# Retention's result turned by VectorE in 32x32 blocks that change places through HBM, with the second attention's branch behind the third gate

## The chip, the cores and the metric

The kernel runs on one core of a Trainium2 chip. The metric is device time in microseconds (us) of one execution; lower is better. Three timed executions of the kernel before gave 818.8, 818.8 and 819.42 us, median 818.8.

## What is computed

A decoder trunk of two layers over 256 tokens of width 1024. In each layer three token mixers run side by side on the normed input: MLA attention, MoBA attention (here one block, so plain causal attention) and retention. Each mixer's result goes through a matrix of its own (its branch), is scaled by a gate of its own, and the three are summed and sent through `w_out`:

```python
merged = (jax.nn.sigmoid(g_mla) * (o_mla @ w_branch_mla)
          + jax.nn.sigmoid(g_moba) * (o_moba @ w_branch_moba)
          + jax.nn.sigmoid(g_ret) * (o_ret @ w_branch_ret))
return merged @ w_out
```

Retention ends in a group norm over each head's 128 columns, a gain and bias, and a silu gate. Then follow a residual, a norm, a squared-ReLU MLP of width 4096 and another residual; after both layers a final norm.

## The kernel before

**Tiles.** The 256 tokens are two row tiles (`t` = 0, 1) of 128 partitions. A matmul contracts over partitions, so whatever is multiplied by a weight must stand turned: features on partitions, tokens along the free axis. Products are of fp32 accuracy: every operand is split into a rounded high part and the rest (`hi`, `lo`), and `three` (L239 to L242) issues three matmuls of 128x512 for each pair.

**Weights.** A weight block (512 KB for most) is loaded by SP into one of seven `raw` buffers (`fetch`, L204), copied by ScalarE into `whi` (L219) and subtracted by VectorE into `wlo` (L221), six buffers each. Every weight block costs each of these two engines one instruction of about a microsecond.

**Order of the work.** `prog` is a list of units that TensorE runs in turn: the three `project` calls of retention (`rqk`, `rv`, `rg`), the branch of MoBA (`bmoba`, two halves of 512 output columns in two units each), the third gate (`gret`, two halves in four units), the branch of retention (`bret`), then `w_out`. Steps hung on a unit with `at(slot(...))` are called behind it in program order. Within that a scheduler with a timeline model sets each engine's order, and each engine then runs its own queue strictly in that order.

**Retention's end.** `ret_values` (L1021 to L1023) leaves the result in two PSUM tiles `por`. `group_norm` takes statistics (L1033, L1034), a power -0.5 on GpSimd (L1036), normalises row tile 0 on VectorE (L1047) and row tile 1 on ScalarE (L1045), and applies gain, bias and gate in two VectorE instructions per row tile (L1051, L1052). The result `oret` stands in rows. `oret_turn` turns it: eight TensorE transposes of 128x128 per layer into PSUM tiles `pot` (L1061), and two splits into `oreth` (ScalarE) and `oretl` (VectorE), L261.

**The branches' sum.** `branch` (L630) multiplies by the branch's weights and then, on VectorE, gates each of four tiles (half, t) with a SCALAR_TENSOR_TENSOR (L650, which also frees the PSUM tile `acc`) and adds it to `merged` (L651). `merged_turn` (L1091, called between the matmuls of `bret1`, whose TensorE order is written out by hand) transposes `merged` on TensorE, four transposes `pmt` (L1097) per tile, for `w_out`.

**The MLP's own turn.** `squared_relu` (L1185) turns its hidden tile in another way: VectorE turns 32x32 blocks (STREAM_TRANSPOSE, L1192), one DMA stores them to a `bounce` buffer in HBM (L1194), four DMAs read them back with the blocks in their new places (L1198), and ScalarE and VectorE split the result (L261). There are eight such trips per layer.

Of the kernel before, what the change touches and what calls it, by code (L numbers as in the profile page):

```python
# [7 lines left out]
F32 = mybir.dt.float32  # L8
# [6 lines left out]
P = 128  # L15
D = 1024
S = 256
NT = S // P
L = 2
KD = D // P  # L20
DFF = 4096
NF = DFF // P

ENDS = [2] * (L - 1) + [4]
LEAD = 10
# [35 lines left out]
def weight_plan():  # L61

    plan = []

    def block(key, name, kt, cols, per):
        for j in range(0, kt, per):
            plan.append(((*key, j // per), name, (j, per), cols))

    def turned(key, cols):
        for n in range(4):  # L70
            block((*key, n), "w_in", KD, cols[P * n : P * n + P], KD)

    def span(c, n):
        return range(c, c + n)

    for l in range(L):
        if l == 0:

            for i in range(2):
                plan.append(((l, "mq", i), "w_in", (0, 1), C_MQ[256 * i : 256 * i + 256]))  # L80
            plan.append(((l, "b0", 0), "w_in", (0, 1), C_MLA))
            for k in range(1, KD):
                plan.append(((l, "b0mq", k), "w_in", (k, 1), [*C_MLA, *C_MQ]))
        else:
            block((l, "b0"), "w_in", KD, C_MLA, 2)
            turned((l, "mq"), C_MQ)
        turned((l, "mk"), C_MK)
        block((l, "mv"), "w_in", KD, C_MV, 2)
        mv, plan = plan[-4:], plan[:-4]
        for i, (key, name, kt, cols) in enumerate(  # L90
            (("qrope", "mla_w_q_up", 2, C_QROPE), ("qnope", "mla_w_q_up", 2, C_QNOPE), ("kvup", "mla_w_kv_up", 1, C_KV))
        ):
            block((l, key), name, kt, cols, kt)
            plan.append(mv[i])
        plan.append(mv[3])
        for i in range(2):
            block((l, "gmla%d" % i), "w_in", KD, span(C_GMLA + 512 * i, 512), 2)
        for i in range(2):
            block((l, "gmoba%d" % i), "w_in", KD, span(C_GMOBA + 512 * i, 512), 2)
        for i in range(2):  # L100
            block((l, "bmla%d" % i), "w_branch_mla", 4, span(512 * i, 512), 2)
        turned((l, "rqk"), C_RQK)
        block((l, "rv"), "w_in", KD, C_RV, 2)
        block((l, "rg"), "w_in", KD, span(C_RG, 512), 2)
        for i in range(2):
            block((l, "bmoba%d" % i), "w_branch_moba", 4, span(512 * i, 512), 2)
        for i in range(2):
            block((l, "gret%d" % i), "w_in", KD, span(C_GRET + 512 * i, 512), 2)
        for i in range(2):
            block((l, "bret%d" % i), "w_branch_ret", 4, span(512 * i, 512), 2)  # L110
        for n in range(KD):
            block((l, "wout", n), "w_out", KD, span(P * n, P), KD)
        for kind, i in mlp_order():
            if kind == "up":
                g, j = divmod(i, 4)
                plan.append(((l, "up", g, j), "w_mlp_up", (2 * j, 2), span(512 * g, 512)))
            else:
                plan.append(((l, "down", i, 0), "w_mlp_down", (i, 1), range(D)))
    at, offset = {}, 0
    for key, name, (j, n), cols in plan:  # L120
        at[key] = (offset, n, len(cols))
        offset += P * n * len(cols)
    return plan, at, offset
# [22 lines left out]
def trunk(ctx: ExitStack, tc: tile.TileContext, gx, wts, consts, gfin, gn, xtok, out):  # L146
# [83 lines left out]
    def misc_tile(name="misc"):  # L230
        return ps.tile([P, 512], F32, name=name, tag="misc", bufs=4)
# [4 lines left out]
    def t4(name):  # L236
        return sb.tile([P, 4, S], F32R, name=name, tag="t4", bufs=T4)
# [24 lines left out]

    def chunk(n):
        return X[n // 4][:, n % 4, :]

    class Normed:

# [359 lines left out]
            project(l, f"{key}{half}", xn, 512, lambda accs, half=half: done(half, accs))  # L627
        return th

    def branch(l, key, oT, th, merged, between=None):  # L630


        def unit(half, j, accs):
# [19 lines left out]
                    merged[half, t] = z  # L653
                    nc.vector.scalar_tensor_tensor(z, z, 1.0, accs[t], op0=ALU.add, op1=ALU.mult)

        for half in range(2):
            accs = []
            for j in range(2):
                prog.append(((f"{key}{half}", j), lambda half=half, j=j, accs=accs: unit(half, j, accs)))
# [46 lines left out]
    def at(slot, step):  # L706
        steps.setdefault(slot, []).append(step)
# [12 lines left out]
    def layer(l, xn, before):  # L720
# [241 lines left out]

        at(slot("gmoba1", 3), load_dec)
        merged, mT = {}, []
        branch(l, "bmla", omlaT, th_mla, merged)
        if l == 0:

            for i, (key, j) in enumerate((("gmoba0", 0), ("gmoba0", 1), ("gmoba1", 0), ("gmoba1", 1))):
# [29 lines left out]
                rqkv["tab"] = tables(xn, rqkv["dec"][:, RT_H * 3 * P :], nc.gpsimd)  # L998
            rT.append(rope_turned(raw, rqkv["tab"], nc.vector))

        rT, or_ps, aT, rg, oret = [], [], {}, {}, []

        def ret_scores():
            banks = [misc_tile("ps_r") for _ in range(RT_H)][::-1]
# [46 lines left out]
                nc.vector.scalar_tensor_tensor(o, o, xn.halfcol[t], gw, op0=ALU.mult, op1=ALU.mult)  # L1051
                nc.vector.scalar_tensor_tensor(o, gb, xn.halfcol[t], o, op0=ALU.mult, op1=ALU.add)  # L1052

        def oret_turn(i):
            if i == 0:
                oretT.extend((t4("oreth"), t4("oretl")))
            pt = misc_tile("pot")
            for kk in range(2):
                k = 2 * i + kk
                for t in range(NT):  # L1060
                    nc.tensor.transpose(  # L1061
                        pt[:, (2 * kk + t) * P : (2 * kk + t + 1) * P], oret[t][:, P * k : P * k + P], ident
                    )
            split_plain(pt, *(o[:, 2 * i : 2 * i + 2, :].rearrange("p k s -> p (k s)") for o in oretT))

        project_turned(l, "rqk", xn, ret_pair)
        project(l, "rv", xn, 512, ret_done("rv"))
# [16 lines left out]

        project(l, "rg", xn, 512, rg_done)
        at(slot("rg", 0), load_gn)
        branch(l, "bmoba", omobaT, th_moba, merged)
        th_ret = gates(l, "gret", xn)
        order_out = ExitStack()

# [15 lines left out]
            else:  # L1106
                merged_turn(0, i - 1)

        branch(l, "bret", oretT, th_ret, merged, between)
        at(slot("rg", 1), lambda: in_a_row(*moba_last, ret_scores))  # L1110
        for h in range(RT_H):
            at(slot("rg", 3), lambda h=h: ret_values(h))
        at(slot("rg", 3), group_norm)
        for i in range(2):
            at(slot("gret0", 3), lambda i=i: oret_turn(i))


        xm = []
# [65 lines left out]

        def squared_relu(g):  # L1185

            blocks = sb.tile([P, 4 * S], F32, name="hblocks", tag="probT", bufs=2)
            for t in range(NT):
                s = w2k("relu")
                nc.scalar.activation(s, us[g][t], AF.Relu, scale=xm.col[t])  # L1190
                nc.scalar.activation(s, s, AF.Square)
                nc.vector.transpose(blocks.rearrange("p (b j t e) -> p t j b e", b=4, j=4, t=2)[:, t], s)  # L1192
            bounce = dr.tile([P, 4 * S], F32, name="hbounce", bufs=2)
            nc.sync.dma_start(bounce, blocks)  # L1194
            turned = sb.tile([P, 4 * S], F32, name="hturned", tag="t4", bufs=T4)
            for b in range(4):
                src = bounce.rearrange("(a p) (b r) -> b p a r", a=4, b=4)[b]
                nc.sync.dma_start(turned[32 * b : 32 * b + 32, :].rearrange("p (a r) -> p a r", a=4), src)  # L1198
            sq = sb.tile([P, 2, 4, S], F32R, name="sq", tag=("Q", "KK")[g % 2], bufs=1)
            src = turned.rearrange("p (a m e) -> p m a e", a=4, e=32)  # L1200
            dst = (sq[:, i].rearrange("p j (t a e) -> p (j t) a e", a=4, e=32) for i in range(2))
            latest[:] = split_plain(src, *dst)
            for j in range(4):
                h2[4 * g + j] = sq[:, 0, j, :], sq[:, 1, j, :]

# [227 lines left out]
```

## Time and profile before

| | before |
|---|---|
| median of three timed runs | 818.8 us |
| the profiled execution, its own time | 819.33 us |
| its span, first to last instruction | 817.2 us |
| TensorE (PE) busy | 810.5 us, 99% |
| VectorE (DVE) busy | 573.4 us, 70% |
| ScalarE (ACT) busy | 459.8 us, 56% |
| GpSimd (POOL) busy | 97.1 us, 12% |
| mean granted TensorE clock | 0.998 |

The profile is of one execution. Busy shares are means over all stages; what limits a stage is read from the stretch itself, and for TensorE from how far apart its matmuls start, since they overlap. Times inside a layer are from the span's start. The two layers repeat the stage that the change touches; the second stands 403.19 us behind the first (its first `bmoba` matmul starts at 563.46, the first layer's at 160.27).

### The profile page before, as it was taken

The page shows a single profiled execution, that of the slowest core. Times are in us where ns is not written, and L with a number is a line of the kernel's source. Part 1 is how long each engine was busy: PE and PEld are TensorE (multiplying, and loading weights), DVE is VectorE, ACT ScalarE, POOL GpSimd, SP SyncE. Part 2 cuts the span into 40 slices and gives each one's busy share as a digit, 9 for nine tenths or more (in the row PEclk, how much of TensorE's full clock was granted, in tenths as well). Part 3 has the DMA queues.
Part 4 walks back from the last instruction along what each step waited for, and adds up shares of the span by engine and source line. Part 5 has one row for each costly group of instructions (what it writes and reads, how often), then busy time and mean ns, then how long its engine had stood idle before and what let it go on. Part 6 is the DMA issues. An engine that isn't in the chain of part 4 may idle for free.

```text
span 817.2 us, 11451 instructions
## 1 busy us (share of the span) xinstructions
PE 810.5 (99%) x4023; PEld 679.8 (83%) x4023; DVE 573.4 (70%) x940; ACT 459.8 (56%) x724; POOL 97.1 (12%) x75
## 2 busy tenths in 40 slices
PE   9999999999999999999999999999999999999997
PEld 7888888888888888888898888888888888888885
DVE  6879699796786455555597976787978744565562
ACT  7676655445555455555586565554555544565552
POOL 0100540330030000000035210013201200000000
PEclk9999999999999999999999999999999999999999
DMA  9964665757476777777656548548575776777731
GB/s 335 346 238 131 243 205 182 265 202 222 143 224 213 241 254 271 249 249 235 205 185 206 190 132 332 165 120 288 163 232 164 242 233 223 257 258 257 243 118 51
DMA packets 62648, 177.94 MB, mean 218 GB/s; under 512 B 8704, under 2 KB 21376, under 8 KB 62336
## 3 DMA queue, kind: packets, MB, share of 16 engines
q1 hardware_dynamic: 61248, 175.77, 64.4%
q10 hardware_dynamic: 1344, 1.46, 0.6%
q8 instruction: 31, 0.51, 0.2%
q14 instruction: 25, 0.20, 0.1%
HBM read 159.37 MB, written 9.44 MB: 207 GB/s over the span
## 4 chain that ended last, share of the span: by engine, by line
PE 99%; DVE 0%; ACT 0%; issue 0%; DVEq 0%
PE acc L242 18%; PE acc L240 18%; PE acc L241 18%; PE pup L241 7%; PE pup L242 7%; PE pup L240 7%; PE acc L1131 5%; PE acc L421 5%; PE acc L423 2%; PE ps_s L947 1%; PE acc L789 1%; PE po L588 1%; PE ps_s L490 1%; PE warm L700 0%; PE acc L791 0%; PE po L590 0%
## 5 line engine op out<-in xcount | busy, mean ns | idle before, releaser
L221 DVE TENSOR_TENSOR wlo<-raw,whi 128x1024 fp32r<-128x1024 f32 (+4 forms) x287 | 342.4, 1212 | 113.1 <-ACT whi L219 110.2
L219 ACT ACTIVATE whi<-raw 128x1024 fp32r<-128x1024 f32 (+4 forms) x287 | 287.6, 1022 | 168.3 <-PE acc L242 92.5
L240 PE MATMUL acc<-whi,xs 128*128 128x512 f32 (+1 forms) x304 | 118.7, 392 | 0.0
L242 PE MATMUL acc<-whi,xs 128*128 128x512 f32 (+1 forms) x304 | 118.4, 390 | 0.0
L241 PE MATMUL acc<-wlo,xs 128*128 128x512 f32 (+1 forms) x304 | 117.8, 387 | 0.0
L240 PE MATMUL acc<-whi,sq 128*128 128x512 f32 x256 | 99.9, 390 | 0.0
L241 PE MATMUL pup<-wlo,xs 128*128 128x512 f32 x256 | 99.8, 390 | 0.0
L242 PE MATMUL pup<-whi,xs 128*128 128x512 f32 x256 | 99.6, 389 | 0.0
L242 PE MATMUL acc<-whi,sq 128*128 128x512 f32 x256 | 99.6, 389 | 0.0
L241 PE MATMUL acc<-wlo,sq 128*128 128x512 f32 x256 | 99.6, 389 | 0.0
L240 PE MATMUL pup<-whi,xs 128*128 128x512 f32 x256 | 99.3, 389 | 0.0
L261 DVE TENSOR_TENSOR sq<-hturned,sq 128x1024 fp32r<-128x1024 f32 x16 | 19.6, 1225 | 77.6 <-ACT sq L261 77.6
L242 PEld LDWEIGHTS acc<-whi,xs 128*128 128x128 f32 x304 | 57.1, 188 | 11.5
L240 PEld LDWEIGHTS acc<-whi,xs 128*128 128x128 f32 x304 | 57.0, 188 | 11.5 <-issue 0.7
L241 PEld LDWEIGHTS acc<-wlo,xs 128*128 128x128 f32 x304 | 57.1, 188 | 10.9
L261 ACT ACTIVATE sq<-hturned 128x1024 fp32r<-128x1024 f32 x16 | 17.0, 1061 | 80.9 <-DMA hturned<-hbounce 80.9
L240 PEld LDWEIGHTS acc<-whi,sq 128*128 128x128 f32 x256 | 48.1, 188 | 10.0
L242 PEld LDWEIGHTS acc<-whi,sq 128*128 128x128 f32 x256 | 48.0, 188 | 10.0
L242 PEld LDWEIGHTS pup<-whi,xs 128*128 128x128 f32 x256 | 48.1, 188 | 9.8
L241 PEld LDWEIGHTS acc<-wlo,sq 128*128 128x128 f32 x256 | 48.1, 188 | 9.8
L241 PEld LDWEIGHTS pup<-wlo,xs 128*128 128x128 f32 x256 | 48.1, 188 | 9.8
L240 PEld LDWEIGHTS pup<-whi,xs 128*128 128x128 f32 x256 | 47.9, 188 | 9.8
(218 smaller groups left out, 1136.7 us busy)
## 6 DMA issues: line engine op xcount, KB each, us to landing
raw<-wts SPq DMA_DIRECT2D x264, 512.0 KB, 4.6
hbounce<-hblocks SPq DMA_DIRECT2D x16, 512.0 KB, 4.5
hturned<-hbounce SPq DMA_DIRECT2D x64, 128.0 KB, 2.9
probT<-blocks SPq DMA_DIRECT2D x80, 48.0 KB, 1.9
qkoth<-qkraw SPq DMA_DIRECT2D x48, 64.0 KB, 2.3
raw<-wts SPq DMA_DIRECT2D x5, 464.0 KB, 6.0
dec<-consts SPq DMA_DIRECT2D x2, 1024.0 KB, 6.3
raw<-wts SPq DMA_DIRECT2D x4, 416.0 KB, 4.1
```

Source lines behind the costliest of these rows:

```text
L219: nc.scalar.activation(hi[:, cs], raw[:, cs], AF.Copy)
L221: nc.vector.tensor_sub(lo[:, cs], raw[:, cs], hi[:, cs].bitcast(F32))
L240: nc.tensor.matmul(o, ah, bh, start=start, stop=False)
L241: nc.tensor.matmul(o, ah, bl, start=False, stop=False)
L242: nc.tensor.matmul(o, al, bh, start=False, stop=stop)
L261: return nc.scalar.activation(hi, src, AF.Copy), nc.vector.tensor_sub(lo, src, hi.bitcast(F32))
L421: nc.tensor.matmul(acc, wh[:, k, :], xn.both(k), start=k == 0, stop=False)
L423: nc.tensor.matmul(acc[:, 0:S], wl[:, k, :], xn.k(k)[0], start=False, stop=k == KD - 1)
L490: mm = nc.tensor.matmul(bank[:, o], a[rows, sa], b[rows, sb_], start=True, stop=True)
L588: nc.tensor.matmul(dst, vh, pT[h + j][0], start=True, stop=False)
L789: nc.tensor.matmul(mq[n], wq[n][0], xn.both(k), start=k == 0, stop=False)
L1131: nc.tensor.matmul(o, a, b, start=half == 0 and i == 0, stop=4 * half + n == KD and i == len(jobs) - 1)
```

## The change

Three things change in every layer, and nothing else. (1) `oret` is turned in the MLP's manner, by code lifted out of `squared_relu` into `turned_blocks` and `split_turned`: two block transposes on VectorE, a store of 512 KB, four reads of 128 KB, and one split of 128x1024 in place of two of 128x512. The eight TensorE transposes are gone. (2) The program's order of units is now `rg`, `gret0`, `gret1`, `bmoba0`, `bmoba1`, `bret0`, `bret1`; the weights are laid out and loaded in that order. (3) The split is called behind unit `bmoba0`, 0.

```diff
+LATE = [(name, half) for name in ("moba", "ret") for half in range(2)]
+SPLIT = "bmoba0", 0
...
         for i in range(2):
-            block((l, "bmoba%d" % i), "w_branch_moba", 4, span(512 * i, 512), 2)
-        for i in range(2):
             block((l, "gret%d" % i), "w_in", KD, span(C_GRET + 512 * i, 512), 2)
-        for i in range(2):
-            block((l, "bret%d" % i), "w_branch_ret", 4, span(512 * i, 512), 2)
+        for name, i in LATE:
+            branch_block(name, i)
...
+    def turned_blocks(rows, name, tag, bufs):
+
+        blocks = sb.tile([P, 4 * S], F32, name=name + "blocks", tag="probT", bufs=2)
+        for t in range(NT):
+            nc.vector.transpose(blocks.rearrange("p (b j t e) -> p t j b e", b=4, j=4, t=2)[:, t], rows[t])
+        bounce = dr.tile([P, 4 * S], F32, name="bounce", bufs=2)
+        nc.sync.dma_start(bounce, blocks)
+        turned = sb.tile([P, 4 * S], F32, name=name + "turned", tag=tag, bufs=bufs)
+        for b in range(4):
+            src = bounce.rearrange("(a p) (b r) -> b p a r", a=4, b=4)[b]
+            nc.sync.dma_start(turned[32 * b : 32 * b + 32, :].rearrange("p (a r) -> p a r", a=4), src)
+        return turned
+
+    def split_turned(turned, parts):
+
+        src = turned.rearrange("p (a m e) -> p m a e", a=4, e=32)
+        return split_plain(src, *(o.rearrange("p j (t a e) -> p (j t) a e", a=4, e=32) for o in parts))
...
-    def branch(l, key, oT, th, merged, between=None):
+    def branch(l, key, parts, oT, th, merged, between=None):
...
-        def oret_turn(i):
-            if i == 0:
-                oretT.extend((t4("oreth"), t4("oretl")))
-            pt = misc_tile("pot")
-            for kk in range(2):
-                k = 2 * i + kk
-                for t in range(NT):
-                    nc.tensor.transpose(
-                        pt[:, (2 * kk + t) * P : (2 * kk + t + 1) * P], oret[t][:, P * k : P * k + P], ident
-                    )
-            split_plain(pt, *(o[:, 2 * i : 2 * i + 2, :].rearrange("p k s -> p (k s)") for o in oretT))
+        def oret_blocks():
+            oret_T.append(turned_blocks(oret, "oret", "probT", 2))
+
+        def oret_split():
+            oretT.extend((t4("oreth"), t4("oretl")))
+            split_turned(oret_T[0], oretT)
...
-        branch(l, "bmoba", omobaT, th_moba, merged)
         th_ret = gates(l, "gret", xn)
...
-        branch(l, "bret", oretT, th_ret, merged, between)
+        branches = {"moba": (omobaT, th_moba), "ret": (oretT, th_ret)}
+        for name, half in LATE:
+            branch(l, "b" + name, [half], *branches[name], merged, between if name == "ret" else None)
...
-        for i in range(2):
-            at(slot("gret0", 3), lambda i=i: oret_turn(i))
+        at(slot("rg", 3), oret_blocks)
+        at(slot(*SPLIT), oret_split)
```

Outside this stage every engine's order is the same as before; line numbers after the change are some 20 higher. Three places, all in the first layer (the second repeats them):

TensorE before, at the seam of the gate's halves `gret0` and `gret1` (`xs` is the normed input, `pot` the PSUM tile of the turn):

```order
L241 MATMUL acc<-wlo,xs_92 128x512
L242 MATMUL acc<-whi,xs_92 128x512
L1061 MATMUL pot<-K,oret 128x128 x2
L240 MATMUL acc<-whi,xs_89 128x512
L241 MATMUL acc<-wlo,xs_89 128x512
```

After the change no row of `pot` is left, and 96 matmuls of the gate stand ahead of the 48 of `bmoba`; the transposes `pmt` of `merged` keep their place among the matmuls of `bret1`.

SP (the queue that issues the loads) after the change, from the load of the group norm's gains on:

```order
L1100 DMA gn<-gn 128x1024
L208 DMA raw<-wts 128x1024 x13
L276 DMA bounce<-oretblocks 128x1024
L208 DMA raw<-wts 128x1024 x2
L280 DMA oretturned<-bounce 32x4x256 x4
L208 DMA raw<-wts 128x1024 x22
```

The store stands behind thirteen weight loads and the four reads behind two more; before, all of these were weight loads in one row.

VectorE before, in the middle of the group norm (`th` are the gates' tiles and `merged`; a `th` fed by an `acc` is L650's gating, a `th` fed by a `th` is L651's sum):

```order
L1047 TENSOR_SCALAR oret_1831<-por_1817,gmv_1833,gve_1834 128x128 x4
L221 TENSOR_TENSOR wlo_2016<-raw_2013,whi_2015 128x1024
L650 SCALAR_TENSOR_TENSOR th_1295<-th_1295,acc_1915 128x512
L1041 SCALAR_TENSOR_TENSOR goff_1865<-gmv_1853,gve_1854 128x4
L1051 SCALAR_TENSOR_TENSOR oret_1831<-oret_1831,half_315,rg_1805 128x512
L650 SCALAR_TENSOR_TENSOR th_1297<-th_1297,acc_1916 128x512
L221 TENSOR_TENSOR wlo_2056<-raw_2053,whi_2055 128x1024
L651 TENSOR_TENSOR th_1000<-th_1000,th_1295 128x512
```

After the change the gating and sums of `bmoba` (eight instructions of 128x512) stand behind the split `oretl`:

```order
L265 TENSOR_TENSOR oretl_2060<-oretturned_1878,oreth_2059 128x1024
L672 SCALAR_TENSOR_TENSOR th_1120<-th_1120,acc_2039 128x512
L225 TENSOR_TENSOR wlo_2150<-raw_2147,whi_2149 128x1024
L672 SCALAR_TENSOR_TENSOR th_1122<-th_1122,acc_2040 128x512
L673 TENSOR_TENSOR th_845<-th_845,th_1120 128x512
L225 TENSOR_TENSOR wlo_2176<-raw_2173,whi_2175 128x1024
L673 TENSOR_TENSOR th_847<-th_847,th_1122 128x512
L225 TENSOR_TENSOR wlo_2194<-raw_2191,whi_2193 128x1024
L672 SCALAR_TENSOR_TENSOR th_1295<-th_1295,acc_2085 128x512
L672 SCALAR_TENSOR_TENSOR th_1297<-th_1297,acc_2086 128x512
L673 TENSOR_TENSOR th_1000<-th_1000,th_1295 128x512
```

and the rest of that row, up to the sum that the first transposes `pmt` read (`th_845` is `merged` of half 0, row tile 0):

```order
L225 TENSOR_TENSOR wlo_2235<-raw_2232,whi_2234 128x1024
L673 TENSOR_TENSOR th_1002<-th_1002,th_1297 128x512
L225 TENSOR_TENSOR wlo_2242<-raw_2239,whi_2241 128x1024
L672 SCALAR_TENSOR_TENSOR th_1957<-th_1957,acc_2127 128x512
L672 SCALAR_TENSOR_TENSOR th_1959<-th_1959,acc_2128 128x512
L673 TENSOR_TENSOR th_845<-th_845,th_1957 128x512
```

So between `oretl` and that sum stand ten instructions of gating and summing and five weight splits; before, only the two gatings of `bret0` stood right ahead of it, those of `bmoba` being long done.

## Rows read from the trace of the kernel before

**Rows 1.** The page: busy time of each engine, us, share of span, instructions.

```profile
PE 810.5 (99%) x4023; PEld 679.8 (83%) x4023; DVE 573.4 (70%) x940; ACT 459.8 (56%) x724; POOL 97.1 (12%) x75
```

**Rows 2.** The page: engines on the chain of work that ended last.

```profile
PE 99%; DVE 0%; ACT 0%; issue 0%; DVEq 0%
```

**Rows 3.** Windows, both gate halves, both layers: length; PE, PEld, DVE, ACT, POOL busy; clock, DMA share, GB/s.

```profile
173.88:184.77 10.89, 10.89 (x49) 8.96 (x48) 10.66 (x18) 6.01 (x9) 1.82 (x2) 1.00 0.43 146
184.77:196.61 11.84, 11.84 (x57) 9.85 (x56) 8.16 (x9) 6.48 (x9) 0.00 (x0) 1.00 0.83 264
577.07:587.96 10.89, 10.89 (x49) 8.96 (x48) 10.06 (x18) 5.90 (x9) 3.16 (x2) 1.00 0.45 145
587.96:599.80 11.84, 11.84 (x58) 9.85 (x56) 9.41 (x10) 6.48 (x9) 0.00 (x0) 1.00 0.78 261
```

**Rows 4.** Timeline of PE, first layer, the turn: start, us, what, count.

```profile
188.22 0.82 PE L1061 MATMUL pot<-K,oret 128*128 128x128 f32 x6
```

**Rows 5.** The tile of the MLP's blocks: ns min/median/max, first and last start.

```profile
L1192 DVE STREAM_TRANSPOSE hblocks<-relu x32: 668/687/712, 245.9 to 787.5; 128x512 f32<-128x512 f32 x32
```

**Rows 6.** Timeline of DVE, the group norm: first layer, then the second layer's first row.

```profile
168.15 0.67 DVE L650 SCALAR_TENSOR_TENSOR th<-th,acc 128x512 f32<-128x512 f32 x1
...
169.85 1.67 DVE L1033 BATCH_NORM_STATS2 gst<-por 128x6 f32<-128x128 f32 x8
171.45 0.36 DVE L1034 BATCH_NORM_AGGREGATE gmv<-gst 128x2 f32<-128x6 f32 x4
171.73 0.65 DVE L650 SCALAR_TENSOR_TENSOR th<-th,acc 128x512 f32<-128x512 f32 x1
...
174.76 1.37 DVE L1047 TENSOR_SCALAR oret<-por,gmv,gve 128x128 f32<-128x128 f32 x4 [0.23 <-POOL gve L1036]
176.04 1.22 DVE L221 TENSOR_TENSOR wlo<-raw,whi 128x1024 fp32r<-128x1024 f32 x1
177.17 0.68 DVE L650 SCALAR_TENSOR_TENSOR th<-th,acc 128x512 f32<-128x512 f32 x1
177.77 0.16 DVE L1041 SCALAR_TENSOR_TENSOR goff<-gmv,gve 128x4 f32<-128x4 f32 x1
177.84 0.75 DVE L1051 SCALAR_TENSOR_TENSOR oret<-oret,half,rg 128x512 f32<-128x512 f32 x1
178.51 0.68 DVE L650 SCALAR_TENSOR_TENSOR th<-th,acc 128x512 f32<-128x512 f32 x1
...
572.04 0.67 DVE L650 SCALAR_TENSOR_TENSOR th<-th,acc 128x512 f32<-128x512 f32 x1
```

**Rows 7.** Timeline of POOL, the power -0.5 of row tile 0, both layers.

```profile
172.86 1.86 POOL L1036 TENSOR_TENSOR gve<-gve,neghalf 128x4 f32<-128x4 f32 x1 [3.48 <-DVE gve L1035]
...
576.76 2.49 POOL L1036 TENSOR_TENSOR gve<-gve,neghalf 128x4 f32<-128x4 f32 x1 [3.48 <-DVE gve L1035]
```

**Rows 8.** Timelines of SP, ACT, DVE: first, slowest and last of the MLP's sixteen trips.

```profile
247.21 0.33 SPq L1194 DMA_DIRECT2D hbounce<-hblocks  x1
...
256.47 1.06 ACT L261 ACTIVATE sq<-hturned 128x1024 fp32r<-128x1024 f32 x1 [4.13 <-DMA hturned<-hbounce]
...
257.56 1.23 DVE L261 TENSOR_TENSOR sq<-hturned,sq 128x1024 fp32r<-128x1024 f32 x1 [3.96 <-ACT sq L261]
...
664.55 0.33 SPq L1194 DMA_DIRECT2D hbounce<-hblocks  x1
...
675.80 1.06 ACT L261 ACTIVATE sq<-hturned 128x1024 fp32r<-128x1024 f32 x1 [4.91 <-DMA hturned<-hbounce]
...
788.21 0.33 SPq L1194 DMA_DIRECT2D hbounce<-hblocks  x1
...
795.12 1.06 ACT L261 ACTIVATE sq<-hturned 128x1024 fp32r<-128x1024 f32 x1 [1.83 <-DMA hturned<-hbounce]
```

**Rows 9.** Timeline of PE, both layers: the first transposes of the sum of branches.

```profile
204.78 0.60 PE L1097 MATMUL pmt<-K,th 128*128 128x128 f32 x4
...
607.97 0.60 PE L1097 MATMUL pmt<-K,th 128*128 128x128 f32 x4
```

More of the change, by code (lines that the diff above doesn't have):

```diff
@@ L99, in weight_plan, with branch_block @@
             block((l, "gmoba%d" % i), "w_in", KD, span(C_GMOBA + 512 * i, 512), 2)
+        def branch_block(name, i):
+            block((l, "b%s%d" % (name, i)), "w_branch_" + name, 4, span(512 * i, 512), 2)
         for i in range(2):
-            block((l, "bmla%d" % i), "w_branch_mla", 4, span(512 * i, 512), 2)
+            branch_block("mla", i)
         turned((l, "rqk"), C_RQK)
@@ L654, in unit @@
                     nc.vector.scalar_tensor_tensor(z, z, 1.0, accs[t], op0=ALU.add, op1=ALU.mult)
-        for half in range(2):
+        for half in parts:
             accs = []
@@ L964, in layer @@
         merged, mT = {}, []
-        branch(l, "bmla", omlaT, th_mla, merged)
+        branch(l, "bmla", range(2), omlaT, th_mla, merged)
         if l == 0:
@@ L999, in ret_pair @@
             rT.append(rope_turned(raw, rqkv["tab"], nc.vector))
-        rT, or_ps, aT, rg, oret = [], [], {}, {}, []
+        rT, or_ps, aT, rg, oret, oret_T = [], [], {}, {}, [], []
         def ret_scores():
@@ L1185, in squared_relu @@
         def squared_relu(g):
-            blocks = sb.tile([P, 4 * S], F32, name="hblocks", tag="probT", bufs=2)
+            rows = [w2k("relu") for _ in range(NT)]
             for t in range(NT):
[L1189 to L1198, printed above, removed]
+                nc.scalar.activation(rows[t], us[g][t], AF.Relu, scale=xm.col[t])
+                nc.scalar.activation(rows[t], rows[t], AF.Square)
             sq = sb.tile([P, 2, 4, S], F32R, name="sq", tag=("Q", "KK")[g % 2], bufs=1)
-            src = turned.rearrange("p (a m e) -> p m a e", a=4, e=32)
-            dst = (sq[:, i].rearrange("p j (t a e) -> p (j t) a e", a=4, e=32) for i in range(2))
-            latest[:] = split_plain(src, *dst)
+            latest[:] = split_turned(turned_blocks(rows, "h", "t4", T4), [sq[:, i] for i in range(2)])
             for j in range(4):
```

## The prediction

> **What bounds the kernel now.** I read the page first: TensorE is busy for 810.5 of 817.2 us, VectorE for 70%, ScalarE for 56% [rows 1]. The chain of work that ended last is 99% TensorE [rows 2]: nothing ends later than it anywhere. So only two things can move the time: work taken from TensorE, and a wait put in front of it. The table by stretches says how dense the stage of the change is: in both gate halves TensorE is busy for the whole of the stretch, at a granted clock of 1.00 of full speed (its 2.4 GHz level), while VectorE fills 8.16 to 10.66 of some 11 us [rows 3]. VectorE is the engine with the least room here, and the reader should keep it in view.
>
> **What is taken from TensorE.** `gret0` and `gret1` have the same 48 matmuls for their halves; the eight transposes `pot` lie in the second. It takes 11.84 us against 10.89, in both layers [rows 3]. The turn thus costs 0.95 us a layer, **1.90 us** in all. That is less than its matmuls' own durations say, since they overlap (six of them show as one piece of 0.82 us) [rows 4]. The order of branch and gate is changed without changing a single product, so the swap itself costs TensorE nothing.
>
> The Trainium skill has a rule against this change: VectorE: DVE Perf Modes, "Rules for kernel authors", gives a 128x128 transpose to TensorE where PSUM will do as its target, because VectorE turns only 32x32 blocks; in its section "The three transpose paths" it puts the TensorE path at 390 ns (bf16). By that figure the sixteen would be worth an estimated 6.2 us; the rows say 1.90, and I go by them.
>
> **What VectorE and the queues get.** Two block transposes of 0.69 us each, at most [rows 5], come to VectorE, and the split is one of 1.23 us. None of that is on the path by itself. What counts is when the turned result is back, and what has queued up on VectorE by then, because all eight gating and summing instructions of `bmoba` now stand behind the split. I work out the first layer on its own clock.
>
> *Start of the trip.* Before, VectorE runs without a gap worth naming from 168.15 on, and `bmoba`'s gating is mixed into the group norm. Without it the list from 168.15 to the second block transpose is: eight statistics 1.60 us and eight aggregations 0.57 (start to start, the second four taken like the first); three weight splits of 1.13; the normalisation 1.28; the offset 0.07; four gain and gate steps of 0.67; two block transposes, 0.60 and 0.69 (0.60 is the pitch of a 128x512 step such as the gating) [rows 5, 6]. Sum 10.9 us, so 179.05. To this comes a wait: GpSimd's power took 1.86 and 2.49 us while VectorE ran two-operand work beside it [rows 7]; now VectorE asks for it after a single weight split of 1.13. I allow 0.7 us of waiting (bounds 0.2 and 1.2). The store then goes out at 179.8; the thirteen weight loads ahead of it on SP are let go by weight splits that VectorE does before the second block transpose. In the second layer VectorE enters the stage 0.70 us later against TensorE (572.04 less 403.19 is 168.85) [rows 6], so 180.5.
>
> *The trip.* The MLP makes the same one sixteen times, from the store's issue to the start of ScalarE's split: 9.26 us the first, 11.25 the slowest, 6.91 the last one, when hardly anything else moves [rows 8]. The median of the sixteen is 9.85. Here the DMA queues were busy for 0.43 of the stretch in which most of the trip would lie [rows 3], so I take a little less, **9.5** (bounds 6.91 and 11.25). The split then starts at 189.3 and 190.0, counted from each layer's own clock.
>
> The Trainium skill (DMA: Bandwidth & Descriptors, "Anatomy of one DMA") puts the fixed part of a DMA at about 2 us, mostly the confirmation of the last byte, heaviest for HBM. For two transfers in a row that is an estimate of 4 us and the data's own time; the last trip of the MLP, 6.91 us, comes nearest to it [rows 8], the other fifteen do not.
>
> *What waits for the trip.* First `bret0`, which reads the split result: without the transposes it would start at 196.61 less 0.95, 195.66 [rows 3]. The split's two parts end about 2.3 us after its start (1.10 to VectorE's start, 1.23) [rows 8], at 191.6: four microseconds early. The turn itself is hidden. The weight loads behind the four reads on SP and the weight copies behind the waiting split on ScalarE are hidden too: the same waits stand in the MLP sixteen times, and TensorE shows no idle time there [rows 2].
>
> Second, and later, the transposes `pmt` of the branches' sum in `bret1`: they stood at 204.78 [rows 9] and would now be due at 203.83. Between the split and the sum they read, VectorE has ten instructions of 0.60 and five weight splits of 1.13 [rows 6], 11.7 us with no gap. From the split's start on ScalarE: 1.10, then 1.13 for `oretl`, 11.7, and 0.68 for the sum itself: 14.6 us. So the sum is ready at 189.3 + 14.6 = 203.9 in the first layer and at 204.6 in the second; with 0.1 us for the signal TensorE waits 0.2 and 0.9 us. That is **1.1 us given back**. After it VectorE has caught up: the transposes of the second half read sums that follow the first with the same spacing as before, and TensorE is later by then.
>
> **Sum.** -1.90 + 1.1 = -0.8 us. The profiled execution took 819.33 us with a span of 817.2, so it would go to 818.5; it stands 0.5 above the median of the three runs, 818.8, and against that I say **818.0**. A measurement can tell about 0.2% of this kernel from no change, 1.6 us: -0.8 lies inside.
>
> **Rivals.**
>
> 1. *Everything is covered.* If the trip takes under 8.8 us, the sum is ready in time in both layers and the whole 1.90 us stays: 816.9. For it: the queues are lighter here than in the MLP [rows 3], and the quickest trip was 6.91 [rows 8]; four of the sixteen were under 8.8, seven under 9.3, which suffices if GpSimd's power costs only the 0.2. This is where the skill's fixed cost of two transfers would lead. Against it: the weight loads ahead of the store and of the reads make the queues busier than they were. Chance 0.34.
>
> 2. *VectorE's queue becomes the bound of `bret1`.* The same mechanism as in the forecast, priced at the far end: a trip of 11.25 us puts the split at 191.05 and 191.75, the sum at 205.65 and 206.35, and TensorE waits 1.9 and 2.6 us. Sum +2.6, 821.4: slower. The point from which it decides is where both waits together exceed the 1.90 saved: a trip of about 9.9 us is even; 10.8 makes the kernel slower by over 0.2%. One of the sixteen trips was so slow, two would be if the power costs 1.2. Chance 0.12.
>
> 3. *The trip is late for `bret0` itself.* TensorE would stand at 195.66. That takes a trip of over 13 us, and none was; its place is included in the upper end, no chance of its own.
>
> **How the numbers follow.** The forecast, a partial cover, takes trips from 8.8 to 10.8 us and times from 817.1 to 820.4; chance 0.54. The likeliest single time is 818.0. For 8 in 10 the range goes down to the fully covered case, 816.7 with a little for noise, and up to a trip of some 10.6 us, 820.0. Chances: faster by over 0.2% 0.34, within 0.2% 0.54, slower by over 0.2% 0.12.
>
> **What would show it.** Right: no row of `pot`; a stretch from the first gate matmul to `bret0` shorter by 0.95 us in each layer; the store about 11.7 us after VectorE's first statistics in each layer, ScalarE's split 9 to 10 us behind it; TensorE waiting for VectorE's sum at the first `pmt`, more in the second layer than in the first, and nowhere else. Wrong: no wait at `pmt` (rival 1), over 1.5 us there in both layers (rival 2), or a wait at `bret0` or for a weight split, which this account has at nothing.

## The result

The changed kernel takes 824.14 us (median of five runs, 822.94 to 826.74) against 818.83 us of the kernel before, measured beside it. The ratio is 1.0064, 95% interval 1.0053 to 1.0075: slower by 5.3 us, where the forecast had 0.8 us faster and its range ended at 820.0. The profiled execution took 824.03 us with a span of 822.1, against 819.33 and 817.2 before.

The page, busy time and the engines on the chain that ended last; they answer to [rows 1, 2]:

```profile
PE 810.4 (99%) x4007; PEld 679.0 (83%) x4007; DVE 572.4 (70%) x942; ACT 460.2 (56%) x722; POOL 98.1 (12%) x75
...
PE 87%; DVE 7%; DMA 3%; issue 1%; ACT 1%; POOL 0%; SPq 0%; DVEq 0%; ACTq 0%
```

TensorE has 16 instructions fewer than before, the transposes, and yet it is as long busy, and only 87% of the chain instead of 99%. VectorE, DMA and ScalarE have come in, so there are now stretches in which TensorE stands still for them. Which ones, the view of TensorE's waits says (us in total, times, longest):

```profile
PE pmt L1113 <- DVE th L673: 4.7, 2, 2.4
...
PE acc L244 <- DVE th L672: 0.4, 1, 0.4
```

One place in both layers: `pmt`, the transposes of the branches' sum. Before, it had no wait [rows 9]. The 0.4 us is at the second `acc` tile of `bret0`, in the second layer alone. The timeline of TensorE with the length of each wait in brackets:

```profile
205.68 1.05 PE L1113 MATMUL pmt<-K,th 128*128 128x128 f32 x4 [2.30 <-DVE th L673]
...
612.80 0.66 PE L1113 MATMUL pmt<-K,th 128*128 128x128 f32 x4 [2.36 <-DVE th L673]
```

The saving is there as well. Windows over the second gate half and over `bmoba`, which now takes its old place; columns as in [rows 3]:

```profile
173.24:184.13 10.89, 10.89 (x50) 9.01 (x48) 9.64 (x11) 7.16 (x11) 0.00 (x0) 1.00 0.57 184
184.13:195.01 10.88, 10.88 (x50) 9.01 (x48) 4.11 (x5) 5.74 (x7) 0.00 (x0) 1.00 0.60 218
```

They are 10.89 and 10.88 us long where the second window of a layer was 11.84, and the second layer's are 10.89. Put together from the starts of TensorE's first matmul at each landmark, us, before and after (the third column is the run `e5_queues_cleared`, below):

| stretch | before | after | e5 |
|---|---|---|---|
| layer 1: `por` to first `bret0` matmul | 31.76 | 30.80 | 30.80 |
| first `bret0` matmul to first `pmt` | 8.17 | 10.67 | 8.17 |
| first `pmt` to first matmul of `w_out` | 3.65 | 5.29 | 3.66 |
| layer 2: `por` to first `bret0` matmul | 31.77 | 30.80 | 30.80 |
| first `bret0` matmul to first `pmt` | 8.17 | 11.40 | 8.16 |
| first `pmt` to first matmul of `w_out` | 3.65 | 3.70 | 3.67 |

After less before: -1.93 for the transposes, +2.50 and +3.23 for the waits, +1.64 and +0.05 behind them, 5.49 in all. The span grew by 4.9, because TensorE reached the first `por` 0.64 us earlier in this execution, and under 0.1 us came elsewhere.

**Where the wait comes from.** The trip in both layers, timelines of SP and ScalarE; it goes from the store's issue to the start of the split:

```profile
179.45 0.33 SPq L276 DMA_DIRECT2D bounce<-oretblocks  x1
180.55 1.46 SPq L208 DMA_DIRECT2D raw<-wts  x2
186.02 1.75 SPq L280 DMA_DIRECT2D oretturned<-bounce  x4
...
191.03 1.06 ACT L265 ACTIVATE oreth<-oretturned 128x1024 fp32r<-128x1024 f32 x1 [5.07 <-DMA oretturned<-bounce]
...
586.72 0.33 SPq L276 DMA_DIRECT2D bounce<-oretblocks  x1
...
591.43 1.75 SPq L280 DMA_DIRECT2D oretturned<-bounce  x4
...
598.15 1.06 ACT L265 ACTIVATE oreth<-oretturned 128x1024 fp32r<-128x1024 f32 x1 [5.80 <-DMA oretturned<-bounce]
```

191.03 - 179.45 is **11.58 us**, 598.15 - 586.72 is **11.43 us**. In the first layer 6.5 us pass from the store's issue to that of the reads, which wait for it to land, and another 5 to the split. From the split on, VectorE's timeline shows the queue that had built up behind it:

```profile
192.12 1.23 DVE L265 TENSOR_TENSOR oretl<-oretturned,oreth 128x1024 fp32r<-128x1024 f32 x1 [4.90 <-ACT oreth L265]
193.27 0.68 DVE L672 SCALAR_TENSOR_TENSOR th<-th,acc 128x512 f32<-128x512 f32 x1
...
203.75 1.28 DVE L672 SCALAR_TENSOR_TENSOR th<-th,acc 128x512 f32<-128x512 f32 x2
204.94 1.29 DVE L673 TENSOR_TENSOR th<-th 128x512 f32<-128x512 f32 x2
```

VectorE stands for 4.90 us at the split's second part, and from there works without a gap to the sum that the first `pmt` reads. That one starts at 204.94; the transposes start at 205.68.

**The 1.64 us behind the first wait.** Windows behind the wait in the first layer, and in the last row behind that in the second:

```profile
205.68:207.00 1.32, 1.32 (x6) 1.22 (x7) 1.32 (x2) 0.23 (x1) 0.00 (x0) 0.55 0.83 289
207.00:208.00 1.00, 1.00 (x4) 0.81 (x3) 1.00 (x2) 0.36 (x1) 0.00 (x0) 0.50 0.07 29
208.00:209.00 1.00, 1.00 (x4) 0.69 (x3) 1.00 (x2) 0.00 (x0) 0.00 (x0) 0.50 0.69 111
209.00:210.00 1.00, 1.00 (x7) 0.87 (x6) 0.77 (x2) 0.21 (x1) 0.00 (x0) 0.89 0.82 332
...
613.00:615.00 2.00, 2.00 (x13) 1.70 (x12) 2.00 (x3) 0.60 (x1) 0.00 (x0) 1.00 0.61 242
```

In the first layer TensorE's granted clock stood at 0.50 to 0.55 of full speed (0.50 is its 1.2 GHz level) for over three microseconds after the wait of 2.30 us; in the second layer, after 2.36 us, it stayed at 1.00.

### The profile page after: what moved, and what is told of

Read it like the earlier page. It is cut to its first block, busy times and chain, and to the rows that moved or that the text cites. A ratio compares the mean times of both kernels' runs of the same rounds, so it can differ in the third digit from the quotient of the medians.

```text
span 822.1 us, 11429 instructions
## 1 busy us (share of the span) xinstructions
PE 810.4 (99%) x4007; PEld 679.0 (83%) x4007; DVE 572.4 (70%) x942; ACT 460.2 (56%) x722; POOL 98.1 (12%) x75
## 4 chain that ended last, share of the span: by engine, by line
PE 87%; DVE 7%; DMA 3%; issue 1%; ACT 1%; POOL 0%; SPq 0%; DVEq 0%; ACTq 0%
PE acc L244 15%; PE acc L246 15%; PE acc L245 15%; PE pup L244 7%; PE pup L245 7%; PE pup L246 7%; PE acc L1149 5%; PE acc L443 5%; DVE wlo L225 3%; PE acc L445 2%; DMA bounce<-oretblocks 1%; PE ps_s L969 1%; DMA oretturned<-bounce 1%; PE acc L811 1%; DMA raw<-wts 1%
## 5 line engine op out<-in xcount | busy, mean ns | idle before, releaser
L244 PEld LDWEIGHTS acc<-whi,xs 128*128 128x128 f32 x304 | 57.0, 188 | 11.5 <-issue 0.7
L246 PEld LDWEIGHTS acc<-whi,xs 128*128 128x128 f32 x304 | 57.1, 188 | 11.5
```

The source lines that it names most:

```text
L244: nc.tensor.matmul(o, ah, bh, start=start, stop=False)
L246: nc.tensor.matmul(o, al, bh, start=False, stop=stop)
```

## Experiments

The theory: the trip is longer than forecast, the split stands on VectorE and ScalarE for it, everything queued behind it is late, and TensorE pays at `pmt`, with a loss of clock on top. The main rival (A in the expectations): the later place of `bmoba` costs by itself. In the expectations "the third branch" is `bret`, and each run's time stands beside runs of the kernel before of the same session, 819.2 to 819.5 us.

**Without the trip (`e1_no_trip`).** The store and the reads are left out, and so the blocks don't change places.

```diff
         for t in range(NT):
             nc.vector.transpose(blocks.rearrange("p (b j t e) -> p t j b e", b=4, j=4, t=2)[:, t], rows[t])
+        if name == "oret":
+            return blocks
         bounce = dr.tile([P, 4 * S], F32, name="bounce", bufs=2)
```

> Left out: the store to HBM and the reads back; the split takes the blocks as VectorE left them, so the 32x32 blocks of retention's result do not change places. Theory (the trip of 11.5 us brings the split late, VectorE's queue stands behind it, and TensorE waits 2.3 us at pmt in each layer, with a fall of the clock after it): no wait at pmt in either layer, clock 1.00 behind it, and only the gain of 2 x 0.95 us is left: 816.9 us, 816.3 to 817.6. Rival A (the later place of the second attention's branch is what costs, whatever turns the result): the wait at pmt stays at over 1.5 us in each layer and the time is 820 us or more. Rival B (VectorE's transposes and what they displace there): 818.5 to 820 us, with VectorE late at the sums.

816.19 us, ratio 0.9967 (0.9954 to 0.998). No wait at `pmt`, mean clock 0.999: rivals A and B are out. With the trip taken out, the whole loss is gone. The time is 0.1 us below the range expected and 0.7 us under the forecast's first rival, in which everything is covered (816.9); where the 0.7 comes from is open.

**The two parts of the change apart (`e4_order_alone`, `e3_turn_alone`).** First the new order with the old TensorE turn, then the new turn with the old order.

```diff
# e4_order_alone (oret_turn is that of the kernel before)
-SPLIT = "bmoba0", 0
+SPLIT = "gret0", 3
...
-        at(slot("rg", 3), oret_blocks)
-        at(slot(*SPLIT), oret_split)
+        for i in range(2):
+            at(slot(*SPLIT), lambda i=i: oret_turn(i))
# e3_turn_alone
-LATE = [(name, half) for name in ("moba", "ret") for half in range(2)]
-SPLIT = "bmoba0", 0
+LATE = [("ret", half) for half in range(2)]
+SPLIT = "gret1", 0
...
+        branch(l, "bmoba", range(2), omobaT, th_moba, merged)
         th_ret = gates(l, "gret", xn)
```

> Only the place of the second attention's branch behind the third gate; retention's result is turned by the 8 transposes of TensorE as before. Theory: no wait at pmt, the same work on TensorE: 818.8 us, 818.2 to 819.4. Rival A (the later place of the branch is what costs): a wait of over 1.5 us at pmt in each layer, 822 us or more.

819.06 us, ratio 0.9998 (0.9989 to 1.0007), no wait but one at the program's start. By itself the order costs nothing that a measurement can tell; rival A is out.

> Only the turn by VectorE and HBM; the second attention's branch stands ahead of the third gate, as in the kernel before. Theory: the gatings and sums of that branch run beside the group norm, so the store goes out later by up to 4 x 0.68 = 2.7 us, the split, due at the same time, comes after the first products of the third branch are due, and TensorE waits there 0.5 to 3 us in each layer instead of at pmt: 818.5 to 824 us. Rival A (the place of the branch is what costs): no wait, 816.9 us.

833.58 us, ratio 1.0173 (1.0159 to 1.0187): the place was as expected, the size was not. TensorE's waits, and the trip in the first layer:

```profile
PE acc L246 <- ACT oreth L267: 12.3, 2, 7.3
```

```profile
187.35 0.33 SPq L278 DMA_DIRECT2D bounce<-oretblocks  x1
...
199.08 1.06 ACT L267 ACTIVATE oreth<-oretturned 128x1024 fp32r<-128x1024 f32 x1 [5.51 <-DMA oretturned<-bounce]
```

With the gatings and sums of `bmoba` among the group norm, and the weight splits between them, the store goes out 7.9 us later than in the changed kernel in the first layer, not 2.7. The trips are 11.73 and 12.54 us, the waits at `bret0` are 5.0 and 7.3 us, and the clock was at 0.50 after both. So the new turn costs less with the new order than without it: the order moves VectorE's work behind the store. The price is that this work then stands behind the split.

**Moving the sums ahead of the split (`e2_sums_first`).**

```diff
-SPLIT = "bmoba0", 0
+SPLIT = "bmoba0", 1
...
-            split_turned(oret_T[0], oretT)
+            with tc.issue_after(sums[-1].ins): split_turned(oret_T[0], oretT)
```

(`sums` collects the instructions of L673; the split is queued behind the second sum of `bmoba0`.)

> The split is issued on VectorE behind the two sums of the second attention's first half; the trip stays. Theory: 2 gatings and 2 sums (2 x 0.68 + 2 x 0.69 = 2.7 us) leave VectorE's queue behind the split, the sum that pmt waits for ends some 2.5 us earlier, the wait of 2.3 us falls below 0.5 us in each layer, and with it the fall of the clock: 817.5 us, 816.7 to 818.5. Rival A (the order of the branches costs by itself): 821 us or more. Rival C (the split's delay only moves: TensorE waits at the first products of the third branch instead): a wait of 1 us or more there in both layers, 820 to 823 us.

827.04 us, ratio 1.0095 (1.0081 to 1.0109): my theory's number missed by 9.5 us; rival C's place was right, and its range ended 4 us too low. The waits of TensorE, and ScalarE's and VectorE's timeline:

```profile
PE acc L246 <- DVE oretl L265: 4.3, 2, 2.1
PE acc L244 <- DVE th L672: 1.2, 1, 1.2
```

```profile
191.19 1.06 ACT L265 ACTIVATE oreth<-oretturned 128x1024 fp32r<-128x1024 f32 x1 [5.02 <-DMA oretturned<-bounce]
...
193.23 1.22 DVE L225 TENSOR_TENSOR wlo<-raw,whi 128x1024 fp32r<-128x1024 f32 x1 [3.93 <-ACT whi L223]
194.37 0.69 DVE L673 TENSOR_TENSOR th<-th 128x512 f32<-128x512 f32 x1
...
197.31 1.22 DVE L265 TENSOR_TENSOR oretl<-oretturned,oreth 128x1024 fp32r<-128x1024 f32 x1
```

The sums stand behind a weight split, `wlo` at 193.23, which waits 3.93 us for ScalarE's copy of that weight; and the copy stands behind `oreth`, which waits for the trip until 191.19. VectorE's own order had been mended, but ScalarE's queue held the same weights back. The split's second part then came at 197.31, five microseconds later than in the changed kernel. The waits add up to 5.5 us; in the second layer the clock was at 0.50 to 0.56 from 604 to 610 us too, and the stretch from `por` to `pmt` grew there, against `e5_queues_cleared` below, by 3.4 us more than its waits of 1.2 and 2.1.

**Clearing both queues (`e5_queues_cleared`).** The weights up to the third branch's second half are copied and split ahead of `oreth` and `oretl`, and so are the sums of `bmoba0`.

```diff
         def oret_split():
             oretT.extend((t4("oreth"), t4("oretl")))
-            split_turned(oret_T[0], oretT)
+            have(WEIGHTS)
+            with ExitStack() as pinned:
+                for ins in (*casts, sums[-1]):
+                    pinned.enter_context(tc.issue_after(ins.ins))
+                split_turned(oret_T[0], oretT)
```

(`WEIGHTS` is 4; `casts` are the two instructions of the weight fetched last; `SPLIT` is `"bmoba1", 0`.)

> The trip stays; the weights of the third branch up to its second half's first block are cast ahead of the split, on ScalarE and on VectorE, and so are the gatings and sums of the second attention's first half. Theory (what stands behind the late split on the two queues is what costs, not the trip itself): the sum that pmt reads ends near 202.3 in the first layer, ahead of 203.4, when it is due; no wait at pmt in either layer, none over 0.3 us at the third branch's first products, no fall of the clock: 816.9 us, 816.2 to 817.6, the time of the kernel without the trip within 0.7 us. Rival C (the trip is too late for the third branch itself): waits of 1 us or more there, 819 us or more. Rival D (the store and the reads slow the weight loads): waits for loads appear in place of the old one, 819 us or more.

817.52 us, ratio 0.9974 (0.9964 to 0.9984). Timelines of SP, ScalarE and VectorE:

```profile
180.52 0.33 SPq L277 DMA_DIRECT2D bounce<-oretblocks  x1
...
192.21 1.06 ACT L266 ACTIVATE oreth<-oretturned 128x1024 fp32r<-128x1024 f32 x1 [3.02 <-DMA oretturned<-bounce]
...
190.37 1.28 DVE L673 SCALAR_TENSOR_TENSOR th<-th,acc 128x512 f32<-128x512 f32 x2
191.56 1.28 DVE L674 TENSOR_TENSOR th<-th 128x512 f32<-128x512 f32 x2
193.30 1.23 DVE L266 TENSOR_TENSOR oretl<-oretturned,oreth 128x1024 fp32r<-128x1024 f32 x1 [0.46 <-ACT oreth L266]
...
202.58 0.68 DVE L674 TENSOR_TENSOR th<-th 128x512 f32<-128x512 f32 x1
```

The trip is as long as in the changed kernel, 11.69 us (11.70 in the second layer). But now the four gatings and sums of `bmoba0` run ahead of the split, the sum that `pmt` reads ends at 203.3, and `pmt` at 204.26 doesn't wait. TensorE shows no wait in either layer: rivals C and D are out. With the trip as it was, it was the queue behind it that cost the time. The time lies in the range expected, but 1.3 us above the run without the trip where 0.7 was expected; the two intervals overlap, and the rest is open.

**Shortening the trip (`e6_loads_held`), and both (`e7_cleared_and_held`).** Three weight loads of `w_out`, which TensorE needs much later, are issued behind the reads: one that went just ahead of the store, two that went between.

```diff
+            for n in range(HELD): behind[l, "wout", n, 0] = [held[-1]]
```

(`HELD` is 2; `held[-1]` is the last of the four reads; the third load follows since SP keeps its order.)

> As the changed kernel, but three weight loads of the output projection, one issued just ahead of the store and two between it and the reads, are issued behind the reads. Theory (the trip is long because its 512 KB share the DMA engines with these loads): the store lands in 4 to 5 us instead of 6.5 in the first layer, the trip shrinks from 11.6 and 11.4 us to 9 to 10 us, and the wait at pmt by as much, to about 0.5 us: 818 to 820 us. Rival E (the trip's length is its own: its number of pieces, its fixed steps): trip and waits stay within 0.5 us of the changed kernel's, 823 to 825 us. Rival F (the held loads come late for the output projection): trip shorter, but a wait at the first products of the output projection, 820 us or more.

819.31 us, ratio 0.9999 (0.999 to 1.0007). The trip and the windows of its two halves, then the changed kernel's in both layers (last two columns: DMA share and GB/s):

```profile
180.25 0.33 SPq L277 DMA_DIRECT2D bounce<-oretblocks  x1
184.07 1.75 SPq L281 DMA_DIRECT2D oretturned<-bounce  x4
...
188.36 1.06 ACT L266 ACTIVATE oreth<-oretturned 128x1024 fp32r<-128x1024 f32 x1 [3.21 <-DMA oretturned<-bounce]
```

```profile
180.25:184.07 3.82, 3.82 (x19) 3.16 (x18) 2.72 (x3) 1.63 (x2) 0.00 (x0) 1.00 0.36 142
184.07:188.36 4.29, 4.29 (x21) 3.55 (x20) 0.72 (x1) 0.69 (x1) 0.00 (x0) 1.00 0.65 158
```

```profile
179.45:185.96 6.51, 6.51 (x31) 5.38 (x30) 3.43 (x3) 3.92 (x5) 0.00 (x0) 1.00 0.94 311
186.02:191.03 5.01, 5.01 (x24) 4.15 (x23) 1.21 (x1) 0.00 (x0) 0.00 (x0) 1.00 0.67 218
...
586.72:591.43 4.71, 4.71 (x23) 3.89 (x22) 3.45 (x3) 2.46 (x4) 0.00 (x0) 1.00 0.83 276
591.43:598.15 6.72, 6.72 (x31) 5.59 (x30) 1.22 (x1) 0.92 (x2) 0.00 (x0) 1.00 1.05 332
```

The trip fell to 8.11 us, and to 7.04 in the second layer; the store landed in 3.8 and 2.6 us instead of 6.5 and 4.7. So 3.5 to 4.4 of its 11.5 us were the company of these three weight loads; which of the three cost how much was not tried. The Trainium skill (DMA: Bandwidth & Descriptors, "Queues, rings and completion order") states that each DMA engine consumes the descriptors of one queue in ring order; by that a store, or a read, is served behind the loads issued before it, and the trace agrees, with these landings. The waits that are left, and VectorE behind `oretl`:

```profile
PE pmt L1116 <- DVE th L675: 0.6, 2, 0.4
PE b L821 <- ACT whi L224: 0.5, 1, 0.5
...
190.98 2.36 DVE L226 TENSOR_TENSOR wlo<-raw,whi 128x1024 fp32r<-128x1024 f32 x2 [0.30 <-ACT whi L224]
```

The second wait stands at 7.7 us, near the program's start, and not in the stage of the change. The trip is 3.5 and 4.4 us shorter, the waits at `pmt` (0.38 and 0.22) by only 1.9 and 2.1. The reason is that VectorE's order moved as well: from `oretl`, at 189.46, to the end of the sum it takes 15.0 us here and 13.5 in the changed kernel, since six weight splits stand in between instead of five, and 0.30 us of waiting. So this is not the short trip alone; with the old order the waits at `pmt` would by these numbers be gone, an estimate that no run tried. Rival E falls, and rival F too: nothing waits at the first products of `w_out`. The time is in the range expected and only equals the kernel before; the median lies 0.8 us above the profiled execution (818.52), and what the other executions lost is open.

> Both edits of the two runs before together. Theory: nothing waits in either, so the shorter trip has nothing left to give: the time of the kernel with cleared queues within 0.5 us, 816.4 to 817.4 us. Rival F: held loads come late, 818 us or more.

816.71 us, ratio 0.9968 (0.9955 to 0.998). It is 2.5 us under the kernel before and 7.4 under the changed kernel. It is also 0.8 us under e5, where at most 0.5 was expected, but the intervals don't tell the two apart. TensorE shows no wait here either.

**A wait without the trip (`e8_delayed_sum`, `e9_shorter_delay`).** On top of e5, three and then two multiplications by 1 on VectorE ahead of the one sum that the first `pmt` reads.

```diff
+                    for _ in range(3 if (key, half, t) == ("bret", 0, 0) else 0): nc.vector.tensor_scalar(z, z, 1.0, None, op0=ALU.mult)
                     sums.append(nc.vector.tensor_add(merged[half, t], merged[half, t], z))
```

> As the kernel with cleared queues, with three multiplications by 1 on VectorE put ahead of the one sum that pmt reads, in each layer, so that TensorE waits there for a reason that has nothing to do with the trip. Theory (a wait at pmt costs itself and, where TensorE's clock falls after it, some 1.6 us more): waits of 2.5 to 3.5 us in both layers, and a stretch at the lower clock behind at least one of them: 822.5 to 826 us, more than the sum of the two waits above the kernel with cleared queues. Rival G (the clock's fall in the first layer of the changed kernel had to do with the traffic or with something else of that run): the time is above the kernel with cleared queues by the two waits alone, clock 1.00 behind them.

828.04 us, ratio 1.0098 (1.0083 to 1.0114). TensorE's waits, and windows behind the wait, first layer and (last row) second:

```profile
PE pmt L1119 <- DVE th L675: 6.4, 2, 3.4
```

```profile
206.00:208.00 2.00, 1.52 (x6) 1.43 (x7) 0.42 (x1) 0.37 (x1) 0.00 (x0) 0.50 0.62 188
208.00:210.00 2.00, 2.00 (x7) 1.42 (x6) 0.69 (x1) 0.22 (x1) 0.00 (x0) 0.50 0.33 133
210.00:212.00 2.00, 2.00 (x8) 1.80 (x7) 1.71 (x3) 0.60 (x1) 0.00 (x0) 0.50 0.00 0
...
615.00:617.00 2.00, 1.98 (x7) 1.79 (x8) 0.26 (x1) 0.60 (x1) 0.00 (x0) 0.53 0.65 193
```

The two waits, 3.01 and 3.38 us, cost 10.5 us against e5. From landmark to landmark 3.15 and 3.54 is the waits, 2.78 and 1.63 the slower clock behind them. (Their sum is 11.1; the profiled execution reached the first `por` 0.94 us earlier than that of e5, and the two differ by 10.2.) That is above the theory's range, because the clock fell in both layers. Rival G is out: the clock fell here behind a wait that has nothing to do with the trip, and in e5, with the same trip and no wait, it did not.

> As the run with the delayed sum, with two multiplications by 1 instead of three. The second one ended at 204.14 there and the sum takes 0.69, so pmt starts near 204.8, where 203.3 would be due: a wait of some 1.4 us in each layer. Theory (the waits of 2.1 us and less seen so far had no lower clock behind them): the time is that of the kernel with cleared queues plus the two waits alone, 817.5 + 2.8 = 820.3 us, 819.5 to 821.3, clock 1.00 behind both. Rival H (any wait at this place lowers the clock): some 1.6 us more in each layer, 822.5 us or more, with stretches at 0.50.

821.04 us, ratio 1.0027 (1.0017 to 1.0036):

```profile
PE pmt L1119 <- DVE th L675: 3.0, 2, 1.5
```

```profile
206.00:208.00 2.00, 2.00 (x12) 1.65 (x12) 1.69 (x3) 0.76 (x2) 0.00 (x0) 1.00 0.68 184
```

Waits of 1.51 and 1.48 us, clock 1.00 behind both; 3.5 us above e5, where the waits alone give 3.0. Rival H, that any wait lowers the clock, is out. But two of the eleven executions took 823.22 and 824.17 us with mean clocks of 0.997 and 0.994, where the other nine, 820.11 to 821.91, have 0.998 or 0.999. Whether the clock fell in them behind these waits no trace shows.

## Why the prediction was wrong

The mechanism was the forecast's; a term was mis-sized, and one was missing. Step by step, the layers' own times on the clock of before:

| step of the prediction | forecast | measured |
|---|---|---|
| transposes saved, per layer | 0.95 us | 0.96 and 0.97 |
| wait for GpSimd's power | 0.7 (0.2 to 1.2) | 0.91 in both |
| store's issue | 179.8, 180.5 | 180.09, 180.96 |
| **trip** | **9.5 (6.91 to 11.25)** | **11.58, 11.43** |
| split's start to the sum's end | 14.6 | 14.6, 14.6 |
| wait at `bret0` | none | none; 0.38 for its second `acc` tile in layer 2 |
| wait at `pmt` | 0.2 and 0.9 | 2.30 and 2.36 |
| TensorE's clock behind a wait | not considered | +1.64 in layer 1 |

**The step that failed is the trip.** With the measured stores and trips in it, the prediction's own sum gives TensorE 2.5 and 3.3 us of delay at `pmt`; the landmarks moved by 2.50 and 3.23. The prediction took "a little less" than the MLP's median of 9.85 us, since the DMA queues were busy for only 0.43 of "the stretch in which most of the trip would lie" [rows 3]. That row ended at 184.77, and the trip was to run from 179.8 to 189.3: half of it lay in the next row, which has 0.83. Nor was either row the right one. They show the kernel before; the change itself adds 1 MB of store and reads, and SP, which stands at the reads until the store has landed, sends two loads at once behind them (from 187.88 and 593.28). In the changed kernel the two halves of the trip have shares of 0.94 and 0.67 in the first layer and of 0.83 and 1.05 in the second. Both trips are longer than all sixteen of the MLP [rows 8], so the end of the range was short as well. The prediction had argued against its first rival that the weight loads ahead of the store and of the reads make the queues busier, and did not put a price on it; `e6_loads_held` did: 3.5 to 4.4 us.

A hint of that price stood in the trace of before. By the order of SP that was known ahead, two weight loads go between the store and the reads. Of the MLP's sixteen trips thirteen have one load there, two have two, and the last has none; SP's timeline behind the first and the slowest store of [rows 8]:

```profile
248.60 0.33 SPq L204 DMA_DIRECT2D raw<-wts  x1
...
665.65 1.46 SPq L204 DMA_DIRECT2D raw<-wts  x2
```

The last trip took 6.91 us, those with one load 8.10 to 10.55, and the two with two loads 10.17 and 11.25. The busy share tells less: over a whole trip of the MLP it is 0.68 to 0.96 (0.42 in the last), and it is 0.89 for one of 8.50 us and 0.94 for that of 11.25. So the first rival's "the queues are lighter here than in the MLP [rows 3]", for which those rows have no figure of the MLP, holds of the row with 0.43 and not of the one with 0.83.

**The missing term is the clock.** The stretches of before stood at 1.00 [rows 3], and TensorE had no wait in them. The sum gave a wait its own length. The wait of 2.30 us cost 1.64 us more, one of 3.01 in e8 2.78.

**Rival 2 was what happened**, with both waits over 1.5 us as its sign said, and with a chance of 0.12. By its own formula a trip of 11.5 us gives 821.9 (0.25 us of trip over its 11.25, in both layers); the clock's 1.64 takes that to 823.5, and the run gave 824.14. Its chance came from one slow MLP trip in sixteen, as if the sixteen were draws of the same trip. The two trips of the new place were 11.58 and 11.43, and 11.69 and 11.70 in e5; with those of e2, e8 and e9 all ten lie from 10.84 to 11.94, above the MLP's median: the value belongs to the place and its neighbours on the queue. (A slip in the first rival: by the prediction's own sum the second layer is covered up to a trip of 8.6 us, not 8.8, which three of the sixteen stay under, not four.)

What held: no other wait came but the 0.38 us, the split is in time for `bret0` (rival 3), and the swap by itself is free (e4). The rule of the Trainium skill (VectorE: DVE Perf Modes, "Rules for kernel authors"), that a 128x128 transpose belongs on TensorE, comes out right for this kernel as changed, and not for e5 and e7, which are 1.7 and 2.5 us under the kernel before. By the figure in its section "The three transpose paths" the sixteen transposes would have been worth an estimated 6.2 us; the rows of after show 1.93. The estimate of 4 us and the data's time for two transfers, after the Trainium skill (DMA: Bandwidth & Descriptors, "Anatomy of one DMA"), rests on a section about DMAs issued from GpSimd, while the ones here are issued from SP; the changed kernel's trips of 11.58 and 11.43 us are far from it, and of this place's trips the one of 7.04 us, with loads held back, comes nearest to it.

## What to carry to other kernels

Where a wait on a DMA is put into an in-order queue, price not the engine's own work but everything queued behind the wait on every engine that waits, and move that ahead of it on all of them: here moving it on VectorE alone made the kernel slower, and on VectorE and ScalarE together turned +5.3 us into -1.7. Take the length of a transfer from the queue as it will be after the change, with the change's own bytes and the loads issued beside it, and from earlier transfers with as many loads beside them; keep loads that nobody needs soon behind it. And give a wait of TensorE more than its length, since its clock may be lower after it.

## What was not expected of the hardware

The clock of TensorE, granted level behind a wait, in the profiled executions: after single waits of 0.22, 0.38, 1.48, 1.51 and 2.1 us it stayed at 1.00; after 3.01, 3.38, 5.0 and 7.34 us it was at 0.50 to 0.61 for three microseconds or longer; of the waits of 2.30 and 2.36 us the first had a lower clock behind it and the second not. In the second layer of `e2_sums_first`, waits of 1.2 and 2.1 us close together had it too. So two executions of one kernel may differ by it: the five runs of the changed kernel have mean clocks of 0.994 to 0.999, the slowest (826.74 us) the lowest and the fastest (822.94) the highest. What decides between 2.30 and 2.36 was not tried.
